# The second layer's injection multiplied inside the first layer norm, gelus by chunk, the context's first scale early, first weights ahead of the tokens

## The chip, the cores and the metric

The kernel runs on 1 core of one Trainium2 chip. The metric is the device time of one execution in microseconds (us), median of a few runs.

Names used below: PE is TensorE's matmul and PEld its weight load, DVE is VectorE, ACT is ScalarE, POOL is GpSimd, SP is SyncE, whose queue issues nearly all of the DMAs.

## What is computed

Two blocks follow one another. The first takes 256 tokens of width 1024 through four layers: a short convolution, a state-space scan (S5), an RWKV recurrence, and a convolution again. After each layer an injection of a second input `p` and a layer norm follow:

```python
def s5_mixer(x, ...):
    u, z = split(x @ w_in)                      # u feeds the scan, z a gate
    y = scan(u) + d_skip * u                    # 64 groups, 64 complex states each
    y = gelu(y)
    y = y * sigmoid(y @ w_glu + b_glu)
    return (y * silu(z)) @ w_out

def first_block(x, p, ...):
    for i in range(4):
        y = mixer[i](x)                         # conv, S5, RWKV, conv
        r = DN_ALPHA * x + y
        r = r + (p[i] @ ple_proj[i]) * sigmoid(r @ ple_gate[i])
        x = layer_norm(r, ln_g[i], ln_b[i])
    return x
```

The second block takes these tokens and a context of 256 tokens, which is an input of its own, through two layers. Each has a half feed-forward (FFN), a mixer in which tokens and context meet, and another half FFN. Each half FFN begins with an RMS norm that is modulated by numbers from a small vector product with `ada_w`:

```python
def half_ffn(h, g, shift, scale, gate, w1, w3, w2):
    hn = h * rsqrt(mean(h * h) + EPS) * g
    return h + 0.5 * gate * ((silu(mod(hn) @ w1) * (mod(hn) @ w3)) @ w2)
```

## The kernel before

**Layout.** Activations lie transposed: 1024 features are 8 chunks of 128 partitions, and the 256 tokens are the free dimension. A linear layer goes by tiles of 128 output features. Each tile has a weight block of 128 x 1024 fp32 (512 KB).

**Products.** An fp32 product is made from three reduced-precision ones: high by high, high by low, low by high. So a weight tile means 24 matmuls (8 chunks of input, 3 products) of 128 x 256. `Net.get` (L598 to L613) brings a weight block: a DMA on SP into the ring `w` of 4 buffers (L605), a copy `whi` on ACT (L606), a subtraction `wlo` on DVE (L607). Only `ssm_in` is left out of this and goes as raw fp32. Sums over features (means, variances) are matmuls with a constant matrix in `cs_base`, also raw fp32. `split` makes the high and low parts of an activation with one ACT and one DVE instruction.

**First block.** `conv` (layer 0) ends in `finish`, which makes `r` and its parts `rs`. Then `ple_norm` runs. It first calls `ple_proj(i)`: `p`'s two chunks are loaded and split, two weight blocks are fetched, and 48 matmuls (8 output chunks, 2 input chunks, 3 products) and 8 ACT copies make `pp`. It then goes through the 8 tiles of `ple_gate`, adds up `total`, takes the mean (`ps_st<-total`, `ps_st<-r`), subtracts it, squares (`sq`), takes the variance (`ps_st<-sq`), and writes the normed `x` (and for layers other than 0 its parts `xs`). Layer 0's call has a function `early`, which starts the phases of the scan (`ssm_m`, on ACT and DVE) while the norm runs.

**The scan.** `ssm` handles 8 chunks as groups, two at a time: a few matmuls (`ps_ca`, `ps_cb`), phase products and a scan on DVE, then matmuls into `ps_st`, and `y` on DVE. When all eight are done come the gelus of the 8 chunks (ACT, which loads a function table first), the splits into `ys_hi` and `ys_lo`, and the 8 tiles of `ssm_glu`.

**Side work and fillers.** Beside the main stream runs a side generator `n.side`: preparation of the scan, the load of the context, and `ada`, which fetches `ada_w` blocks through the same ring `w` and reduces each with one DVE instruction into `junk` (L1384). From the end of the scan on, the first FFN of the context (`ffn_in00`, `ffn_out`) is woven into the first block as filler: a tile of it (operands `h_hi`, `h_lo`, `d_hi`, `d_lo`) can run wherever the main stream waits. Its first step is `norm_mod`, with the squares of the context (`squares`), their sum, and `h_hi`, `h_lo`. After the first block the two streams, tokens and context, are woven together to the end.

**What sets the order.** The kernel plans itself: `weave` steps whichever stream is ready by a model of the engines' clocks (`Model`, `Engine`), with `yield` values as the expected delay of a step. The tile scheduler then orders the instructions of each engine by priority. Each engine, and SP's queue, runs its list in order.

Of the kernel before, what the change touches and what calls it, by code (L numbers as in the profile page):

```python
# [9 lines left out]
F32 = mybir.dt.float32  # L10
F32R = mybir.dt.float32r
# [8 lines left out]
S = 256  # L20
# [4 lines left out]
RAW = ("ssm_in",)  # L25

# [416 lines left out]
class Net:  # L443
    def __init__(self, tc, ap, pat, cat, es):
# [27 lines left out]
        self.sums = {}  # L472
        self.hold = 0
        self.fine = False
# [120 lines left out]
    def get(self, req):  # L595
# [3 lines left out]
        w = self.ws.tile([128, 1024], F32, name="w")  # L599
# [5 lines left out]
        nc.sync.dma_start(out=w[:, :n], in_=self.ap[name][i])  # L605
# [165 lines left out]
    def ple_proj(self, i):  # L771

        nc = self.nc
        raw = f"ple_proj{i}" in RAW
        t = self.slot(9, [2, 2, S], "p_split", F32 if raw else F32R)
        pp = self.slot(10, [NCH, S], "pp")
        for k in range(2):
            pf = t[:, 0, k] if raw else self.tmp("te")
            nc.sync.dma_start(out=pf, in_=self.ap["pT"][i][:, k])
            if not raw:  # L780
                self.split(pf, t[:, 0, k], t[:, 1, k])
        yield from self.linear(f"ple_proj{i}", t[:, 0] if raw else (t[:, 0], t[:, 1]), lambda m, ps: self.A.activation(out=pp[:, m], in_=ps, func=AF.Copy), 2, 4)
        return pp

    def ple_norm(self, R, i, split=True, free=2, early=None):
# [3 lines left out]
        pp = yield from self.ple_proj(i)  # L789
# [145 lines left out]
    def phases(self, c, q_, make):  # L935
# [4 lines left out]
        if q_ not in self.sets:  # L940
            self.sets[q_] = tuple(self.slot(k, [2048], f"ssm_m{k}") for k in ((6, 7), (0, 1))[q_])
# [20 lines left out]
    def ssm(self, X):  # L962
# [28 lines left out]
        y = full(10, "y")  # L991
# [3 lines left out]
        free = list(range(2))  # L995
        halves = lambda t: t.rearrange("p (t r) -> p r t", r=2)
# [3 lines left out]
        def group(c):  # L1000
# [37 lines left out]
            V.scalar_tensor_tensor(out=halves(y[:, c]), in0=halves(u[:, c]), scalar=self.p("ssm_d", c), in1=yp, op0=MUL, op1=ADD)  # L1038

# [7 lines left out]
        raw = "ssm_glu" in RAW  # L1047
        ys = y if raw else self.pair(0, 1, "ys")
        for c in range(NCH):
            self.tc.keep_in_program_order(self.act(y[:, c], y[:, c], AF.Gelu_apprx_tanh))  # L1050
            if not raw:
                self.split(y[:, c], ys[0][:, c], ys[1][:, c])
        yield 4.0
# [920 lines left out]
```

## Time and profile before

| | us |
|---|---|
| median of 3 runs | 2878.42 (2876.4 to 2881.57) |
| the profiled execution | 2878.2 |
| its span | 2876.3 |
| PE busy in the span | 2738.9 (95%) |
| DVE busy | 2130.2 (74%) |
| ACT busy | 1596.7 (56%) |

The profiled execution takes 1.9 us more than its span, and is 0.2 us under the median. PE is busy nearly all of the time, so the 137 us in which it is not, and the stretches in which it runs at half clock, are what there is to see. A busy time of PE counts a matmul from its start to its modelled end, so at half clock it is busy too. The slices of the page show where PE's share falls: at the start, around 170 to 330 us, and around 520 to 700 us.

### The profile page before, as it was taken

Reading aid. Unit: us, or ns where it says so; the run is one execution under the profiler, and the core shown is the slowest. Engines: PE = TensorE matmul, PEld = TensorE weight load, DVE = VectorE, ACT = ScalarE, POOL = GpSimd, SP = SyncE. Lnnn points to the kernel's source line nnn. Section 1 sums busy time; section 2 is a strip of 40 time slices with the busy share of each in tenths; the row PEclk is TensorE's granted clock in tenths of the full one; section 3 lists DMA queues with packets and bytes.
Section 4 is the critical chain, followed back from the end, with each engine's and each line's share of the span. In section 5 each row is a group of like instructions: output and inputs, shape, how many; then the busy total and the mean of one; then the engine's idle time right before and its main releaser. Section 6 shows DMA issues by size and latency. Waiting matters only on the chain.

```text
span 2876.3 us, 58509 instructions
## 1 busy us (share of the span) xinstructions
PE 2738.9 (95%) x23798; PEld 2587.5 (90%) x23798; DVE 2130.2 (74%) x3951; ACT 1596.7 (56%) x2946; POOL 13.0 (0%) x40
## 2 busy tenths in 40 slices
PE   8978799899999999999999999999999999999999
PEld 8967699778998998998999968999999999996999
DVE  8867777666688788898889887777854556676654
ACT  6455555866655465877666766545422234466443
POOL 0000000000000000000000000000000000000000
PEclk9989799999999999999999999999999999999999
DMA  7743355201486665666575644666544433322554
GB/s 273 244 158 111 107 169 176 82 17 41 159 263 226 221 200 176 211 215 202 182 231 186 201 134 150 209 219 208 176 140 133 132 112 109 94 91 62 160 183 140
DMA packets 132749, 467.51 MB, mean 163 GB/s; under 512 B 14720, under 2 KB 19072, under 8 KB 131840
## 3 DMA queue, kind: packets, MB, share of 16 engines
q1 hardware_dynamic: 132480, 463.78, 50.3%
q8 instruction: 187, 3.06, 0.4%
q14 instruction: 82, 0.67, 0.1%
HBM read 462.67 MB, written 1.05 MB: 161 GB/s over the span
## 4 chain that ended last, share of the span: by engine, by line
PE 68%; DVE 13%; DMA 9%; ACT 6%; issue 4%; SPq 0%; DVEq 0%; ACTq 0%
PE ps_mm L436 58%; DMA w<-in_ada_dram 6%; PE ps_ca L436 5%; DVE wlo L607 4%; PE ps_cb L436 2%; DVE junk L1384 2%; ACT whi L606 2%; DVE ssm_m L406 2%; PE ps_st L436 2%; DVE tc L406 1%; PE ps_cb L440 1%; DMA w<-in_ab_in_dram 1%; ACT rw_b L406 1%; ACT L406 1%; DMA w<-in_ffn_in_dram 1%
## 5 line engine op out<-in xcount | busy, mean ns | idle before, releaser
L606 ACT ACTIVATE whi<-w 128x1024 fp32r<-128x1024 f32 (+1 forms) x687 | 716.0, 1043 | 738.1 <-PE ps_mm L436 476.0
L607 DVE TENSOR_TENSOR wlo<-w,whi 128x1024 fp32r<-128x1024 f32 (+1 forms) x687 | 826.0, 1204 | 249.7 <-ACT whi L606 247.0
L436 PE MATMUL ps_mm<-h_hi,whi 128*128 128x256 f32 x3024 | 871.4, 290 | 16.8 <-ACT h_hi L406 12.9
L436 PE MATMUL ps_mm<-h_hi,wlo 128*128 128x256 f32 x3024 | 857.8, 285 | 6.0 <-DVE wlo L607 5.8
L436 PE MATMUL ps_mm<-h_lo,whi 128*128 128x256 f32 x3024 | 855.7, 284 | 1.1 <-DVE h_lo L406 1.0
L436 PEld LDWEIGHTS ps_mm<-h_hi,whi 128*128 128x128 f32 x3024 | 571.9, 190 | 27.2 <-ACT h_hi L406 16.4
L436 PEld LDWEIGHTS ps_mm<-h_lo,whi 128*128 128x128 f32 x3024 | 575.2, 190 | 6.0 <-DVE h_lo L406 2.8
L436 PEld LDWEIGHTS ps_mm<-h_hi,wlo 128*128 128x128 f32 x3024 | 572.8, 190 | 8.5 <-DVE wlo L607 7.8
L1384 DVE SCALAR_TENSOR_TENSOR junk<-w,cond 128x1024 bf16<-128x1024 f32 x288 | 351.7, 1221 | 149.9 <-DMA w<-in_ada_dram 148.8
L436 PE MATMUL ps_mm<-d_hi,whi 128*128 128x256 f32 x1232 | 355.5, 289 | 3.6 <-DVE ctx L406 2.7
L436 PE MATMUL ps_mm<-d_hi,wlo 128*128 128x256 f32 x1232 | 349.6, 284 | 0.6 <-DVE wlo L607 0.6
L436 PE MATMUL ps_mm<-d_lo,whi 128*128 128x256 f32 x1232 | 349.6, 284 | 0.4 <-DVE d_lo L406 0.4
L436 PEld LDWEIGHTS ps_mm<-d_hi,whi 128*128 128x128 f32 x1232 | 232.1, 188 | 8.0 <-issue 5.4
L436 PEld LDWEIGHTS ps_mm<-d_lo,whi 128*128 128x128 f32 x1232 | 233.3, 189 | 3.4 <-issue 1.2
L436 PEld LDWEIGHTS ps_mm<-d_hi,wlo 128*128 128x128 f32 x1232 | 232.6, 189 | 1.6 <-DVE wlo L607 0.8
L406 DVE TENSOR_TENSOR td<-td,ps_mm 128x256 f32<-128x256 f32 x154 | 64.4, 418 | 71.8 <-PE ps_mm L436 70.6
L406 ACT ACTIVATE d_hi<-td 128x256 fp32r<-128x256 f32 x154 | 63.1, 410 | 90.5 <-DVE td L406 89.7
L406 ACT ACT_TABLE_LOAD x80 | 102.6, 1283 | 2.1 <-PEq L1965 0.7
L436 PE MATMUL ps_mm<-x_hi,whi 128*128 128x256 f32 x256 | 73.9, 289 | 10.7 <-ACT whi L606 10.7
L406 ACT ACTIVATE tc<-tc 128x256 f32<-128x256 f32 x182 | 75.0, 412 | 5.2 <-DVE tc L406 2.4
L436 PE MATMUL ps_mm<-xs_hi,whi 128*128 128x256 f32 x256 | 73.3, 287 | 4.8 <-ACT xs_hi L406 4.6
L406 ACT ACTIVATE td<-ps_mm 128x256 f32<-128x256 f32 x154 | 57.4, 374 | 32.7 <-PE ps_mm L436 32.2
(466 smaller groups left out, 5233.8 us busy)
## 6 DMA issues: line engine op xcount, KB each, us to landing
w<-in_ffn_in_dram SPq DMA_DIRECT2D x268, 512.0 KB, 4.0
w<-in_ada_dram SPq DMA_DIRECT2D x168, 512.0 KB, 4.3
w<-in_ffn_out_dram SPq DMA_DIRECT2D x96, 512.0 KB, 4.0
w<-in_conv_in_dram SPq DMA_DIRECT2D x64, 512.0 KB, 4.7
w<-in_ffn_out_dram SPq DMA_DIRECT2D x48, 384.0 KB, 3.1
w<-in_ab_in_dram SPq DMA_DIRECT2D x34, 512.0 KB, 4.2
w<-in_ple_gate_dram SPq DMA_DIRECT2D x32, 512.0 KB, 4.3
w<-in_conv_out_dram SPq DMA_DIRECT2D x16, 512.0 KB, 4.8
```

Of the source, the lines that this page charges most:

```text
L406: return f(**kw)
L436: self.t.matmul(out, lhsT=lhsT, rhs=rhs, start=start, stop=stop)
L440: self.t.transpose(out, in_, ident)
L606: nc.scalar.activation(out=hi[:, :n], in_=w[:, :n], func=AF.Copy)
L607: nc.vector.tensor_tensor(out=lo[:, :n], in0=w[:, :n], in1=hi[:, :n].bitcast(F32), op=ALU.subtract)
L1384: nc.vector.scalar_tensor_tensor(out=self.junk, in0=w, scalar=1.0, in1=cb[:, s], op0=ALU.mult, op1=ALU.mult, accum_out=m[:, t, s:s + 1])
```

## The change

Five things are changed.

- `FIRST`: the DMA of the first weight block (`conv_in0`, tile 0) is issued ahead of the four DMAs of `x`.
- `ple_split` is taken out of `ple_proj`. In layer 0's norm (`early` is given) the injection of layer 1 is made: `p[1]` is split and its two weight blocks are fetched ahead of the mean, and the 48 matmuls and 8 copies into `pp` are emitted between the squares and the variance. Layer 1's `ple_norm` finds `pp` ready. Since `pp` then holds slot 10 during the scan, the scan's `y` takes the place of `u`, and the two sets of phase buffers swap places.
- The gelus and splits of the scan's result are emitted per chunk inside `group`, from the seventh finished chunk on.
- `context_scale` makes the context's first RMS scale in the side chain, ahead of `ada`: 8 squares on ACT, 8 raw fp32 matmuls against the mean matrix, the rsqrt. `norm_mod` uses it and leaves out its own squares and sums that first time.
- The output is stored by two DMAs, seven chunks and one, instead of one.

```diff
+FIRST = ("conv_in0", 0)
@@ get
-        w = self.ws.tile([128, 1024], F32, name="w")
+        w = self.ws.tile([128, 1024], F32, name="w") if not self.ahead else self.ahead.pop()
...
-        nc.sync.dma_start(out=w[:, :n], in_=self.ap[name][i])
+        if (name, i) != FIRST:
+            nc.sync.dma_start(out=w[:, :n], in_=self.ap[name][i])
@@ ple_norm
-        pp = yield from self.ple_proj(i)
+        pp = self.pp.pop(i) if i in self.pp else (yield from self.ple_proj(i))
...
         if early is not None:
             early()
+
+            ps_ = self.ple_split(i + 1)
+            ws = []
+            for b in range(2):
+                ws.append((yield (f"ple_proj{i + 1}", b, 2, 512)))
         yield 1.5
...
+        if early is not None:
+            self.pp[i + 1] = np_ = self.slot(10, [NCH, S], "pp")
+            for m in range(NCH):
+                ps = self.ps()
+                yield from self.mm3g(ps[:, :S], ws[m // 4], ps_, m % 4)
+                self.A.activation(out=np_[:, m], in_=ps[:, :S], func=AF.Copy)
         yield 3.5
@@ phases
-            self.sets[q_] = tuple(self.slot(k, [2048], f"ssm_m{k}") for k in ((6, 7), (0, 1))[q_])
+            self.sets[q_] = tuple(self.slot(k, [2048], f"ssm_m{k}") for k in ((0, 1), (6, 7))[q_])
@@ ssm
-        y = full(10, "y")
+        y = u
...
+            summed.append(c)
+
+            if len(summed) >= NCH - 1:
+                if not ys:
+                    ys.extend(self.pair(0, 1, "ys"))
+                for k in [k for k in summed if k not in gated]:
+                    gated.add(k)
+                    self.tc.keep_in_program_order(self.act(y[:, k], y[:, k], AF.Gelu_apprx_tanh))
+                    self.split(y[:, k], ys[0][:, k], ys[1][:, k])
...
-        ys = y if raw else self.pair(0, 1, "ys")
-        for c in range(NCH):
-            self.tc.keep_in_program_order(self.act(y[:, c], y[:, c], AF.Gelu_apprx_tanh))
-            if not raw:
-                self.split(y[:, c], ys[0][:, c], ys[1][:, c])
-        yield 4.0
+        yield 1.5
@@ context_scale, norm_mod
+        ms = self.ps("st")[:, :S]
+        for k in range(NCH):
+            t = self.tmp("tc")
+            self.A.activation(out=t, in_=self.ctx[:, k], func=AF.Square)
+            self.T.matmul(ms, lhsT=self.c("mean"), rhs=t, start=k == 0, stop=k == NCH - 1)
+        rs = self.few.tile([128, S], F32, name="rs")
+        self.V.tensor_copy(out=rs, in_=self.rsqrt(ms, 1e-6))
+        self.rs[1] = rs
...
+        if s in self.rs:
+            rs = self.rs.pop(s)
+            self.hold += 1
+        else:
...
@@ program
+        n.ahead = [n.ws.tile([128, 1024], F32, name="w")]
+        nc.sync.dma_start(out=n.ahead[0], in_=ap[FIRST[0]][FIRST[1]])
         X = Stream(n, n.first())
...
-        n.side = itertools.chain(n.ssm_prep(), load_context(), n.ada(c, [(0, i, (1,), GAPS[0] / 2) for i in range(PARTS)]))
+        n.side = itertools.chain(n.ssm_prep(), load_context(), n.context_scale(), n.ada(c, [(0, i, (1,), GAPS[0] / 2) for i in range(PARTS)]))
...
-        nc.sync.dma_start(out=out, in_=x)
+        nc.sync.dma_start(out=out[:, :7], in_=x[:, :7])
+        nc.sync.dma_start(out=out[:, 7:], in_=x[:, 7:])
```

Since the planner's clocks see other costs, the order of the engines' lists changes in more places than the diff. Three of them matter below.

PE's list in layer norm 0. The last products of `ple_gate0` (`rs_hi`, `rs_lo`) stand ahead of the mean (`total`, `r`), the variance (`sq`) and the first raw matmuls of `ssm_in` (`x,w`). Before:

```order
L436 MATMUL ps_mm<-rs_lo,whi 128x256
L436 MATMUL ps_mm<-rs_hi,wlo 128x256
L436 MATMUL ps_st<-total,cs_base 128x256
L436 MATMUL ps_st<-r,cs_base 128x256
L436 MATMUL ps_st<-sq,cs_base 128x256 x3
L436 MATMUL ps_mm<-x,w 128x256 x12
```

After, the same place:

```order
L437 MATMUL ps_mm<-rs_hi,wlo 128x256
L437 MATMUL ps_mm<-p_split,whi 128x256 x2
L437 MATMUL ps_mm<-p_split,wlo 128x256
L437 MATMUL ps_mm<-p_split,whi 128x256 x2
L437 MATMUL ps_st<-total,cs_base 128x256
L437 MATMUL ps_mm<-p_split,wlo 128x256
L437 MATMUL ps_mm<-p_split,whi 128x256 x2
L437 MATMUL ps_mm<-p_split,wlo 128x256
L437 MATMUL ps_mm<-p_split,whi 128x256 x2
```

Five matmuls of the injection now stand ahead of `total`, 25 between `total` and `r`, and 18 between `r` and `sq`.

ACT's list at the end of the scan. `sz` is the scan's gate, `tc` a temporary of the context's norm, `y` (after: `u`) the scan's result under gelu. Before:

```order
L406 ACTIVATE sz<-ps_mm 128x256
L406 ACTIVATE squares<-ctx 128x256 x8
L397 ACT_TABLE_LOAD
L406 ACTIVATE tc<-ps_mm,fixed_66 128x256
L406 ACTIVATE tc<-tc 128x256 x2
L406 ACTIVATE h_hi<-tc,mod 128x256 x8
L406 ACT_TABLE_LOAD
L406 ACTIVATE y<-y 128x256
L406 ACT_TABLE_LOAD
L406 ACTIVATE td<-ps_mm 128x256
L406 ACTIVATE ys_hi<-y 128x256
L406 ACT_TABLE_LOAD
```

After:

```order
L407 ACTIVATE h_hi<-tc,mod 128x256 x3
L407 ACTIVATE sz<-ps_mm 128x256
L407 ACT_TABLE_LOAD
L407 ACTIVATE u<-u 128x256
L407 ACTIVATE ys_hi<-u 128x256
L407 ACTIVATE u<-u 128x256
L407 ACTIVATE ys_hi<-u 128x256
```

The squares are gone from here, three of the context's eight `h_hi` stand ahead of the gelus, and the pairs of gelu and split follow one another eight times with one table load ahead of them.

SP's list over the scan's end, from the raw weights of `ssm_in` on. Before:

```order
L601 DMA w<-in_ssm_in_dram 128x1024 x16
L1381 DMA w<-in_ada_dram 128x1024 x2
L605 DMA w<-in_ffn_in_dram 128x1024
L605 DMA w<-in_ssm_glu_dram 128x1024 x7
L513 DMA rwkv_c<-in_const_rwkv_dram 128x1088
L605 DMA w<-in_ssm_glu_dram 128x1024
L605 DMA w<-in_ffn_in_dram 128x1024 x2
```

After:

```order
L603 DMA w<-in_ssm_in_dram 128x1024 x16
L1401 DMA w<-in_ada_dram 128x1024
L608 DMA w<-in_ssm_glu_dram 128x1024
L1401 DMA w<-in_ada_dram 128x1024
L608 DMA w<-in_ssm_glu_dram 128x1024 x2
L1401 DMA w<-in_ada_dram 128x1024
L608 DMA w<-in_ssm_glu_dram 128x1024 x2
L1401 DMA w<-in_ada_dram 128x1024
L515 DMA rwkv_c<-in_const_rwkv_dram 128x1088
L608 DMA w<-in_ssm_glu_dram 128x1024 x2
L1401 DMA w<-in_ada_dram 128x1024
L608 DMA w<-in_ssm_glu_dram 128x1024
```

Five blocks of `ada` instead of two now stand among the `ssm_glu` weights, in the ring of four that both share.

## Rows read from the trace of the kernel before

**Rows 1.** The page: busy time by engine, and the weights' low part on DVE.

```profile
PE 2738.9 (95%) x23798; PEld 2587.5 (90%) x23798; DVE 2130.2 (74%) x3951; ACT 1596.7 (56%) x2946; POOL 13.0 (0%) x40
...
L607 DVE TENSOR_TENSOR wlo<-w,whi 128x1024 fp32r<-128x1024 f32 (+1 forms) x687 | 826.0, 1204 | 249.7 <-ACT whi L606 247.0
```

**Rows 2.** Windows (stretch and its us, busy by engine, granted clock, DMA share, GB/s).

```profile
102.30:171.60 69.30, 67.58 (x553) 66.76 (x551) 54.13 (x94) 32.64 (x53) 0.10 (x1) 0.98 0.71 235
171.60:193.00 21.40, 5.00 (x10) 2.90 (x10) 15.08 (x37) 13.14 (x31) 0.00 (x0) 0.68 0.39 129
...
303.00:327.30 24.30, 16.75 (x113) 12.33 (x105) 14.62 (x31) 13.22 (x25) 4.45 (x9) 0.57 0.08 24
...
868.60:885.10 16.50, 10.42 (x77) 9.65 (x77) 14.37 (x34) 11.43 (x23) 0.00 (x0) 0.93 0.64 213
1110.00:1800.00 690.00, 671.57 (x5046) 619.00 (x5046) 601.25 (x1177) 484.85 (x852) 0.00 (x0) 0.99 0.60 190
```

**Rows 3.** Timeline of the start (start, us, engine, what, idle before and its releaser).

```profile
0.74 1.81 SPq L712 DMA_DIRECT2D x<-in_xT_dram  x4
...
9.60 1.06 ACT L606 ACTIVATE whi<-w 128x1024 fp32r<-128x1024 f32 x1 [0.70 <-DMA w<-in_conv_in_dram]
...
10.71 0.58 PE L436 MATMUL ps_mm<-x_hi,whi 128*128 128x256 f32 x1 [10.71 <-ACT whi L606]
```

**Rows 4.** Timeline of PE in layer norm 0.

```profile
177.98 1.22 PE L436 MATMUL ps_st<-total,cs_base 128*128 128x256 f32 x2 [6.39 <-DVE total L406]
178.99 1.06 PE L436 MATMUL ps_st<-r,cs_base 128*128 128x256 f32 x2
186.66 2.93 PE L436 MATMUL ps_st<-sq,cs_base 128*128 128x256 f32 x6 [6.61 <-DVE sq L406]
193.03 5.19 PE L436 MATMUL ps_mm<-x,w 128*128 128x256 f32 x15 [3.44 <-ACT x L406]
```

**Rows 5.** Windows in layer norm 0 and at the scan's end, columns as above.

```profile
176.20:180.20 4.00, 2.07 (x4) 1.06 (x4) 3.23 (x9) 0.63 (x1) 0.00 (x0) 0.51 0.87 295
...
193.00:196.70 3.70, 3.67 (x9) 2.94 (x10) 2.20 (x6) 2.77 (x7) 0.00 (x0) 0.54 0.00 0
...
313.30:321.00 7.70, 7.53 (x24) 5.72 (x24) 5.91 (x14) 4.81 (x10) 0.00 (x0) 0.50 0.01 2
321.00:327.20 6.20, 3.30 (x12) 2.71 (x12) 1.95 (x4) 6.10 (x11) 0.00 (x0) 0.50 0.00 0
327.30:329.80 2.50, 2.50 (x11) 2.50 (x12) 1.51 (x5) 2.40 (x8) 0.00 (x0) 0.50 0.62 198
329.80:334.00 4.20, 4.20 (x36) 4.20 (x36) 1.28 (x3) 2.21 (x5) 0.00 (x0) 0.99 0.02 9
```

**Rows 6.** The chain of waits around layer 1's injection (start, us, what).

```profile
371.99 18.05 PE ps_mm L436 x149
```

**Rows 7.** The chain of waits at the end of the scan.

```profile
308.23 1.65 PE ps_mm L436 x4
...
319.25 1.28 ACT L406
320.54 0.01 issue
320.55 0.42 ACT y L406
...
327.29 4.74 PE ps_mm L436 x28
```

**Rows 8.** DMA issues: count, KB each, median us to landing.

```profile
w<-in_ssm_glu_dram SPq DMA_DIRECT2D x8, 512.0 KB, 3.7
...
p<-in_cd_bias_dram SPq DMA_DIRECT2D x16, 128.0 KB, 2.1
...
out_dram<-x SPq DMA_DIRECT2D x1, 1024.0 KB, 3.9
```

**Rows 9.** The chain of waits in the third layer norm.

```profile
874.88 0.45 PE ps_st L436 x2
...
879.20 3.60 DMA w<-in_conv_in_dram
```

More of the change, by code (lines that the diff above doesn't have):

```diff
@@ L471, in __init__ @@
         self.parts, self.stage = [[0, 0], [0, 0]], ""
-        self.sums = {}
+        self.sums, self.rs = {}, {}
         self.hold = 0
+        self.pp = {}
         self.fine = False
@@ L773, in ple_proj, with ple_split @@
         nc = self.nc
-        raw = f"ple_proj{i}" in RAW
-        t = self.slot(9, [2, 2, S], "p_split", F32 if raw else F32R)
+        t = self.ple_split(i)
         pp = self.slot(10, [NCH, S], "pp")
+        yield from self.linear(f"ple_proj{i}", t, lambda m, ps: self.A.activation(out=pp[:, m], in_=ps, func=AF.Copy), 2, 4)
+        return pp
+    def ple_split(self, i):
+        t = self.slot(9, [2, 2, S], "p_split", F32R)
         for k in range(2):
-            pf = t[:, 0, k] if raw else self.tmp("te")
-            nc.sync.dma_start(out=pf, in_=self.ap["pT"][i][:, k])
-            if not raw:
-                self.split(pf, t[:, 0, k], t[:, 1, k])
-        yield from self.linear(f"ple_proj{i}", t[:, 0] if raw else (t[:, 0], t[:, 1]), lambda m, ps: self.A.activation(out=pp[:, m], in_=ps, func=AF.Copy), 2, 4)
-        return pp
+            pf = self.tmp("te")
+            self.nc.sync.dma_start(out=pf, in_=self.ap["pT"][i][:, k])
+            self.split(pf, t[:, 0, k], t[:, 1, k])
+        return t[:, 0], t[:, 1]
     def ple_norm(self, R, i, split=True, free=2, early=None):
@@ L1046, in ssm @@
         yield 1.0
-        raw = "ssm_glu" in RAW
-        ys = y if raw else self.pair(0, 1, "ys")
-        for c in range(NCH):
-            self.tc.keep_in_program_order(self.act(y[:, c], y[:, c], AF.Gelu_apprx_tanh))
-            if not raw:
-                self.split(y[:, c], ys[0][:, c], ys[1][:, c])
-        yield 4.0
+        yield 1.5
         g = self.operand("ssm_out", (2, 3), "g")
@@ L1062, in take_g @@
             self.put(g, m, th, lambda o: V.scalar_tensor_tensor(out=o, in0=th, scalar=0.5, in1=sz[:, m], op0=MUL, op1=MUL))
-        yield from self.linear("ssm_glu", ys, take_g)
+        yield from self.linear("ssm_glu", tuple(ys), take_g)
         yield 1.5
@@ L1401, in modulation, with context_scale @@
                 yield Until(self.now() + 2.0)
+    def context_scale(self):
+        ms = self.ps("st")[:, :S]
[6 more added lines that the diff above has]
+        self.rs[1] = rs
+        yield 3.0
     def norm_mod(self, l, g, i, x, s):
@@ L1408, in norm_mod @@
         self.V.scalar_tensor_tensor(out=ga, in0=self.mod[:, l, (i + 1) * NCH:(i + 2) * NCH, s], scalar=1.0, in1=self.p("norm_g", (l * 3 + g) * NCH, NCH), op0=ALU.add, op1=ALU.mult)
-        if s not in self.sums:
-            for k in range(NCH):
-                self.square(s, k, x[:, k], 4 * s + 2)
-            yield 2.5
-        sq = self.sums.pop(s)
-        ms = self.bsum(self.c("mean"), lambda k: sq[:, k * (NCH - 1)], 2)
-        rs = self.rsqrt(ms, 1e-6)
+        if s in self.rs:
+            rs = self.rs.pop(s)
+            self.hold += 1
+        else:
+            if s not in self.sums:
+                for k in range(NCH):
+                    self.square(s, k, x[:, k], 4 * s + 2)
+                yield 2.5
+            sq = self.sums.pop(s)
+            ms = self.bsum(self.c("mean"), lambda k: sq[:, k * (NCH - 1)], 2)
+            rs = self.rsqrt(ms, 1e-6)
         hi, lo = self.pair(4 * s, 4 * s + 1, f"h{s}")
```

1 line of the change is left out of this document (added).

## The prediction

> **What bounds the kernel now.** The busy times come first: PE is busy 95% of the span, DVE 74% [rows 1]. Of 2876.3 us PE is idle 137, so a change pays in three ways: it takes matmuls away, it fills a gap of PE with matmuls that are done later now, or it spares PE a stretch at half clock, which counts as busy. The windows come second, because the average hides where these gaps lie [rows 2]: 16.4 us of 21.4 in layer norm 0, 7.6 of 24.3 at the scan's end, 6.1 of 16.5 in the third norm, but only 1.7 of 69.3 ahead of norm 0 and 18.4 of 690 in the large woven stretch after 1110 us. The granted clock is the other half: at the scan's end it is 0.50 (1.2 GHz) from 313.3 to 329.8 us, although PE is busy most of that time, and full (2.4 GHz) right after [rows 5]. The chain of waits then says what the gap is made of: at the scan's end the context's norm, the function tables and the gelus stand one behind another from 308.2 to 327.3 us [rows 7].
>
> At full clock the chain shows 149 matmuls back to back in 18.05 us [rows 6]: 0.121 us each, 2.9 us for a weight tile of 24. At half clock 11 of them fill 2.50 us [rows 5]: 0.23 us each.
>
> **The change part by part**, against the profiled execution's 2878.2 us (the median of the runs is 0.2 us above it).
>
> *First weights ahead.* Before, the first matmul starts at 10.71 us, waiting for `whi`, which waits for the weight's DMA; that DMA stands on SP behind the 1.81 us of `x`'s issues [rows 3]. Ahead of them it can land up to 1.8 us earlier, and `whi` (1.06 us) no longer stands at the end of the start; `x` itself lands later, and the next weights come no sooner. Ends: -2.9 and 0. I take -1.9.
>
> *Context's scale early.* It adds eight raw fp32 matmuls. The nearest row is a mean's pair of records, 0.45 us [rows 9], so 8 x 0.45 = 3.6 us. The order of PE puts them between the tiles of `conv_out`, a stretch with 1.7 us of idle in 69.3 [rows 2], so little covers them. Ends: 0 (they fall into waits for weights) and +3.6; I take +3.0. The eight squares on ACT are free there: ACT is busy 32.64 of 69.30 us.
>
> *The injection inside norm 0.* Removed: 48 matmuls at 0.121 = 5.8 us, from a stretch in which PE has no gap at all [rows 6], so all of it counts. The two weight blocks move along, and that only helps the later stretch. Added: the same 48 in norm 0, whose idle 16.4 us could hold them even at half clock (48 x 0.23 = 11.0). But PE takes its list in order, and 25 of them stand between the two halves of the mean, which in the profile of before follow one another [rows 4]. The mean, and all that hangs on it (centring, squares, variance), comes later by 25 x 0.121 = 3.0 to 25 x 0.23 = 5.8 us; the middle is 4.4. ACT is busy 13.14 of 21.40 us there, much of it with the scan's phases, which can go ahead while the mean is late; I let half be absorbed: +2.2. The eight copies into `pp` are some 0.42 us each (the ACT step of the same 128 x 256 shape in [rows 7]); the order leaves three of them between the last square and the logarithm's table load: at most 1.3, taken as 0.8. Against that, a PE that has worked may keep its clock. The variance's 2.93 us and the first 3.7 us of `ssm_in` run at 0.50 and 0.54 of the clock before [rows 4, 5]; at full clock they would be 1.5 and 1.8 us shorter. I take -1.0 of these. So norm 0 grows by 2.0 and the part is -5.8 + 2.0 = -3.8; ends -9.1 (everything warm, nothing late) and +1.3.
>
> *Gelus by chunk, and the context's norm off the end of the scan.* Before, PE's last group ends at 308.2 us and from there to 329.8 us it does the context's sums, then 24 + 12 + 11 = 47 matmuls, all at half clock [rows 5, 7]: 24 of the context's tile, 23 of `ssm_glu`. After, seven of eight chunks have passed gelu when the last group ends, and some of the context's operands are ready, so these 47 can follow at once. With 3.7 us at half clock first, as `ssm_in` needs after norm 0 [rows 5], that is 16 matmuls, and 31 more at 0.121: 7.5 us in all, done at 315.7 instead of 329.8. That is -14.1; with a warm PE it is 5.7 us and -15.9. What is late next is a weight. Five blocks of `ada` now stand among those of `ssm_glu` in the ring of four, and each frees its buffer only after a DVE step that queues behind the scan on DVE. A step of this ring in the open is: the DVE step (1.2 us; the row of `wlo`, same tile, taken for it), landing 3.7 [rows 8], `whi` 1.06 [rows 3], `wlo` 1.2 [rows 1]: 7.2 us, of which one tile of 2.9 covers part. I count one such exposure, 4.3, since four blocks can be there before the need begins: -14.1 + 4.3 = -9.8. Ends: -15.9 and, with all of the last four tiles exposed, +3.
>
> Here the trace speaks against a page. A table load takes 1.28 us and the next ACT instruction starts 0.02 us behind it [rows 7]. The Trainium skill (page "ScalarE: Activation LUTs", section "What ACT_TABLE_LOAD costs") adds a drain of about 1.38 us to each, 2.66 in all. The order of ACT has two loads fewer in this place; by the page they would save another 2 x 1.38 = 2.8 us and the forecast would be some 2857. By the row they save nothing beyond what the -14.1 holds, and I go by the row.
>
> *More filler done early.* The order now holds one context tile more in the RWKV scan (-2.9) and two more in the third norm (-5.8, against 6.1 us of idle there [rows 2]). But there the first `conv_in` weights are split only after the normed operands; before, a weight's landing (3.60 us, [rows 9]) and `whi` (1.06) lay among the norm's steps. If they come into the open, that is +4.7. Net -4.0; ends -8.7 and +4.7.
>
> *Output in two.* The last transfer shrinks from 1024 KB, 3.9 us, to 128 KB, for which the nearest row has 2.1 us [rows 8]. The large part starts a tile (2.9 us) earlier and is over. -1.8; ends -2.0 and 0.
>
> *The woven rest.* Its order changes in many places but the work is the same. PE idles 18.4 us in its largest stretch [rows 2], which a re-ordering can give or take in part: 0, ends -8 and +8.
>
> Sum: -1.9 + 3.0 - 3.8 - 9.8 - 4.0 - 1.8 + 0 = -18.3, so 2878.2 - 18.3 = 2859.9, say 2860 us. Taken together (root of squares of the half-widths, about 14), the ends give 2846 to 2874.
>
> **The rivals.**
>
> *The gain is given back.* The ring behind `ada` exposes each of the last four `ssm_glu` tiles (4 x 4.3 = 17.2, so that part gives +3 instead of -9.8): 2860 + 13 = 2873. If the weave returns a few microseconds as well, up to 2880. For it: DVE is the one that frees the ring and is the scan's own engine. Against it: 47 matmuls of cover stand ready, and the context's tiles can run in between. About no change.
>
> *Slower through the large woven stretch.* With four to five context tiles done before it instead of about two, the context's and the token stream's serial steps (norms, attention) may come at the same time, with no filler left for either. PE is busy 671.57 of 690 us there and DVE 601.25 [rows 2]; a DVE at 87% can become the bound in parts. It ends slower than before once that stretch loses over 24 us (18.3 + 5.8), 3.5% of it; at 5%, 34 us, the time is 2894. For it: DVE's share. Against it: the fillers that are missing there were done in idle time earlier, so the stretch has less work by the same amount.
>
> *The injection does not pay.* The mean is late by the whole 5.8 us with nothing absorbed, and the clock stays at half: norm 0 grows by 7.1, the part is +1.3 instead of -3.8: 2865.
>
> *More than forecast.* PE stays warm from norm 0 on and no weight is exposed: -5.3 in norm 0, -6.1 at the scan's end: 2849.
>
> **How the numbers follow.** Chances: the forecast 0.45, the injection that doesn't pay 0.15, more than forecast 0.13, given back 0.17, slower through the weave 0.10. About 0.2%, 5.8 us, is what a measurement of this kernel tells from no change: faster means under 2872.7, slower over 2884.2. So faster 0.73, same 0.17, slower 0.10. The range of 8 in 10 leaves out the slower case and a part of the ends: 2844 to 2877.
>
> **What would show each step.** Norm 0: `ps_st<-r` behind 25 matmuls of `p_split`, ending near 184 us rather than 180, and `ssm_in` starting about 195 at a higher clock. At 380 us no matmuls of `p_split`. The scan's end: no stretch of 16 us at 0.50; the first `ssm_glu` matmuls ahead of the last group; PE's waits for `wlo` of `ssm_glu` at most one of about 4 us. The third norm: more matmuls between its mean and its variance. The end: the last store lands about 2 us after its issue. The forecast is wrong if the offset between equal instructions of the two traces, about 14 us at the first `ssm_out` tile and about 20 at the end of the third norm, shrinks again after 1110 us; or if PE waits for several `ssm_glu` weights in a row.

## The result, and the profile after

The changed kernel takes 2860.32 us (median of four runs, 2859.29 to 2864.55), the kernel before 2879.99 us beside it: a ratio of 0.9931, with a 95% interval of 0.9911 to 0.9951. The forecast was 2860.0. The execution that was profiled is the slowest of the four, 2864.55 us, of which the span is 2862.7: 13.6 us shorter than that of before, where the medians differ by 19.7.

The page's busy times hardly move against [rows 1]; PE is idle 127 us of the span instead of 137:

```profile
PE 2735.5 (96%) x23810; PEld 2589.5 (90%) x23810; DVE 2128.4 (74%) x3947; ACT 1591.5 (56%) x2944; POOL 13.0 (0%) x40
```

The start, in order of time, answers to [rows 3]. The first matmul comes at 6.90 instead of 10.71 us and waits for the tokens' split `x_hi`, no longer for the weight:

```profile
0.74 0.38 SPq L1949 DMA_DIRECT2D w<-in_conv_in_dram  x1
1.18 1.84 SPq L715 DMA_DIRECT2D x<-in_xT_dram  x4
...
4.33 1.06 ACT L609 ACTIVATE whi<-w 128x1024 fp32r<-128x1024 f32 x1 [2.32 <-DMA w<-in_conv_in_dram]
...
6.90 0.58 PE L437 MATMUL ps_mm<-x_hi,whi 128*128 128x256 f32 x1 [6.90 <-ACT x_hi L407]
```

PE in layer norm 0, which answers to [rows 4]. The injection (`p_split`, not shown) fills the stretch from `total` to `r`, which is now 4.43 us long instead of 1.01; the trace has 21 of its matmuls there and 22 behind `r`, where 25 and 18 were read from the order; the variance (`sq`) still takes 2.93 us:

```profile
172.88 0.70 PE L437 MATMUL ps_st<-total,cs_base 128*128 128x256 f32 x2 [2.51 <-DVE total L407]
...
177.31 0.71 PE L437 MATMUL ps_st<-r,cs_base 128*128 128x256 f32 x2
185.95 2.93 PE L437 MATMUL ps_st<-sq,cs_base 128*128 128x256 f32 x6 [5.20 <-DVE sq L407]
```

The scan's end, in windows with the columns of [rows 2]: layer norm 0 first, then the end of the raw weights, and then two stretches that answer to [rows 5]. Before, the granted clock was 0.50 (1.2 GHz) for 16.5 us there; now PE is full and at full clock (2.4 GHz) from 310 to 322 us:

```profile
169.80:192.30 22.50, 11.37 (x58) 9.72 (x57) 14.44 (x37) 16.82 (x40) 0.00 (x0) 0.75 0.34 121
...
291.30:310.00 18.70, 10.87 (x165) 8.23 (x166) 18.13 (x39) 9.59 (x24) 4.45 (x9) 0.73 0.23 75
310.00:322.00 12.00, 12.00 (x102) 12.00 (x101) 11.81 (x25) 7.57 (x15) 0.00 (x0) 1.00 0.46 143
322.00:334.30 12.30, 10.90 (x75) 10.30 (x74) 10.40 (x19) 6.55 (x12) 0.96 (x1) 0.87 0.74 233
```

The chain of waits there answers to [rows 7] (start, us, what). Norm, tables and gelus are gone from it. What stands in it is one weight of `ssm_glu`, issued only when a `wlo` on DVE has ended:

```profile
307.82 11.36 PE ps_mm L437 x93
...
320.12 1.23 DVE wlo L610
...
321.40 5.29 DMA w<-in_ssm_glu_dram
...
328.81 1.23 DVE wlo L610
```

The RWKV scan, from its first matmul to the first of `rwkv_out`, before and then after, the same columns. It holds 22 weight tiles of the context before and 23 after:

```profile
524.30:807.70 283.40, 266.69 (x3858) 230.90 (x3857) 188.18 (x432) 181.47 (x467) 1.10 (x1) 0.98 0.24 78
```

```profile
508.10:799.70 291.60, 273.49 (x3883) 236.47 (x3882) 189.05 (x435) 187.70 (x474) 1.10 (x1) 0.97 0.24 79
```

It is 8.2 us longer, and one tile of 24 matmuls explains 2.9 of these.

The chain at the end of the third norm answers to [rows 9]: it goes through the first `conv_in` weight and both of its splits. The landing stood on the chain before, too.

```profile
878.88 3.50 DMA w<-in_conv_in_dram
...
882.46 1.06 ACT whi L609
...
883.55 1.24 DVE wlo L610
```

The end. The last two stores and how long they take (KB, median us from issue to landing), against 1024 KB in 3.9 us [rows 8]:

```profile
out_dram<-x SPq DMA_DIRECT2D x1, 896.0 KB, 3.8
out_dram<-x SPq DMA_DIRECT2D x1, 128.0 KB, 2.0
```

**The leads.** The table gives how many us earlier than in the trace of before the same place is reached, at equal work: 2.9 us are added for each tile of the context that is done more by then, and taken off for each done less. e1 is a second run of the changed kernel; the other columns are the experiments below. The trace of before belongs to a run of 2878.2 us, and the kernel before has a median of 2875.9 to 2879.2 in the later comparisons, so that leads at the end exceed the timed gains by up to 2.3 us for that alone.

| place | after | e1 | e2 | e3 | e4 | e5 | e8 | e10 | e11 |
|---|---|---|---|---|---|---|---|---|---|
| `ple_gate0` over | 1.8 | 0.0 | 2.4 | 1.1 | 1.4 | 0.9 | 1.1 | 1.0 | 4.8 |
| `ssm_in` begins | 0.7 | 1.6 | 1.8 | 2.0 | -2.0 | -1.3 | -1.1 | -1.4 | 4.5 |
| `ssm_in` over | 0.2 | 2.0 | 1.7 | 2.1 | -2.4 | -0.5 | -0.1 | -1.4 | 5.4 |
| second norm's mean | 18.7 | 22.9 | 0.4 | 18.6 | 14.4 | 13.8 | 19.6 | 18.2 | 25.2 |
| RWKV scan begins | 19.0 | 22.1 | 0.6 | 18.7 | 14.2 | 12.7 | 19.5 | 18.0 | 24.9 |
| `rwkv_out` begins | 13.8 | 16.0 | 0.3 | 14.3 | -2.3 | 8.4 | 12.0 | 18.0 | 24.1 |
| second `conv_in` over | 13.6 | 20.1 | 1.7 | 17.9 | -0.6 | 12.0 | 10.1 | 22.1 | 25.3 |
| end | 13.6 | 22.0 | 1.3 | 19.6 | 4.2 | 15.5 | 10.3 | 23.2 | 32.6 |

### The profile page after: what moved, and what is told of

It is laid out like the page before. It is cut to its first block, busy times and chain, and to the rows that moved or that the text cites. A ratio compares the mean times of both kernels' runs of the same rounds, so it can differ in the third digit from the quotient of the medians.

```text
span 2862.7 us, 58511 instructions
## 1 busy us (share of the span) xinstructions
PE 2735.5 (96%) x23810; PEld 2589.5 (90%) x23810; DVE 2128.4 (74%) x3947; ACT 1591.5 (56%) x2944; POOL 13.0 (0%) x40
## 4 chain that ended last, share of the span: by engine, by line
PE 66%; DVE 14%; DMA 9%; ACT 7%; issue 4%; SPq 0%; ACTq 0%; DVEq 0%
PE ps_mm L437 55%; PE ps_ca L437 5%; DMA w<-in_ada_dram 4%; DVE wlo L610 4%; PE ps_cb L437 3%; ACT whi L609 2%; PE ps_st L437 2%; DVE junk L1404 2%; DVE ssm_m L407 2%; DVE tc L407 2%; DMA w<-in_ffn_in_dram 1%; DMA w<-in_conv_in_dram 1%; PE ps_cb L441 1%; ACT tc L407 1%; ACT L407 1%
## 5 line engine op out<-in xcount | busy, mean ns | idle before, releaser
L437 PE MATMUL ps_mm<-h_hi,whi 128*128 128x256 f32 x3024 | 871.8, 289 | 13.8 <-ACT h_hi L407 5.7
L437 PEld LDWEIGHTS ps_mm<-h_hi,wlo 128*128 128x128 f32 x3024 | 571.4, 189 | 10.1 <-DVE wlo L610 9.6
L437 PE MATMUL ps_mm<-xs_hi,wlo 128*128 128x256 f32 x256 | 74.0, 289 | 3.7 <-DVE wlo L610 3.7
```

Of the source, the lines that this page charges most:

```text
L437: self.t.matmul(out, lhsT=lhsT, rhs=rhs, start=start, stop=stop)
```

## The experiments

Each ratio is to the kernel before, on the same chip and beside it, with its 95% interval.

**e1, the changed kernel once more**, with no edit.

> The changed kernel, unaltered, for a second profile: the profiled execution (2864.5 us) lay 4 us above the median of its runs (2860.3). Theory: the planned order is the same, so the first block runs alike to within 1 us (first matmul 6.9 us, last matmul of ssm_glu 334.3, first of rwkv_out 799.7, variance of the fourth norm 1049.1) and the 4 us arise after 1110 us, where two streams share the weights' ring; ratio to the kernel before 0.9931 again. Rival: the first block itself differs by some us between executions, for instance in the RWKV stretch, and then the 10.7 us that the change's lead loses there (508 to 800 us) is partly chance: rwkv_out would start 3 us or more earlier than 799.7.

0.9932 [0.9915, 0.9949], 2855.86 against 2876.01 us. The gain repeats. But two executions of the same lists of instructions differ by 4.2 us of lead at the second norm, so a lead of one execution is good to about that; the theory had expected the first block alike to within 1 us. The loss in the RWKV scan repeats: 6.1 us of lead against 5.2.

**e2, only the two ends**: the kernel before with the first weight ahead and the output in two.

```diff
+FIRST = ("conv_in0", 0)
...
+        n.ahead = [n.ws.tile([128, 1024], F32, name="w")]
+        nc.sync.dma_start(out=n.ahead[0], in_=ap[FIRST[0]][FIRST[1]])
...
-        nc.sync.dma_start(out=out, in_=x)
+        nc.sync.dma_start(out=out[:, :7], in_=x[:, :7])
+        nc.sync.dma_start(out=out[:, 7:], in_=x[:, 7:])
```

> The kernel before with the two ends of the change alone: first weight block issued ahead of the tokens, output stored by two transfers. The planner sees neither, so every engine's order stays that of before. Theory: the start's gain (3.2 us through conv_in in the changed kernel, where 1.9 was forecast) and the end's (2.2 us, where 1.8 was forecast) are real and add: conv_in's tiles begin 3.2 us earlier all the way to 85 us, the last store is 3.0 us ahead of the span's end instead of 5.2, and the time falls by 5.4 us (ratio 0.998). Rival: the start's lead is spent where weights are late anyway (conv_out and norm 0 in the changed kernel kept only 0.7 us of lead), so that only the end's 2.2 us stay: ratio 0.9992.

0.9993 [0.998, 1.0005], 2873.12 against 2876.01 us: not to be told from nothing, and near the rival's 0.9992. The lead of 2.4 us at the end of `ple_gate0` is 0.4 at the second norm: what the start gains is gone by the end of the selective scan.

**e3, the injection back in layer 1's norm.**

```diff
-            ps_ = self.ple_split(i + 1)
-            ws = []
-            for b in range(2):
-                ws.append((yield (f"ple_proj{i + 1}", b, 2, 512)))
...
-        if early is not None:
-            self.pp[i + 1] = np_ = self.slot(10, [NCH, S], "pp")
-            for m in range(NCH):
-                ps = self.ps()
-                yield from self.mm3g(ps[:, :S], ws[m // 4], ps_, m % 4)
-                self.A.activation(out=np_[:, m], in_=ps[:, :S], func=AF.Copy)
```

> The changed kernel with the injection of layer 1 made in its old place (the first step of layer 1's norm), all else as changed. Theory: the 48 matmuls cost their full 5.8 us there (layer 1's first gate matmul loses 5.7 us of its lead) and layer norm 0 gives back about 1 us, so up to the second layer norm the kernel stands 4.6 us behind the changed one; the planner then also places fewer early tiles of the context (40, 43 and 45 by the third and fourth norm instead of 44, 47 and 49), which costs some us more. Ratio to before 0.9945 to 0.996. Rival: the injection's 5.8 us reappear as waits anyway, the lead of the changed kernel is lost in the RWKV stretch, and the time is within 2 us of the changed one (0.993).

0.9946 [0.9927, 0.9964], 2860.63 against 2875.89 us: 4.0 us of gain less than e1 by the ratios (0.0014 x 2876), though the intervals overlap. The traces do not settle what the move is worth. The removed matmuls show in full: between the last product of `ssm_out` and the first of `ple_gate1` lie 5.7 us before and 5.8 in e3, and nothing in after (366.0 and 365.9 us). But from the end of `ssm_in` to that last product e3 gains 16.4 us, where the changed list gains 12.8, 15.3, 14.0 and 14.0 (after, e1, e8, e10), and e3 passes norm 0 0.9 us faster than before, the changed list mostly 1.1 to 2.4 slower. So at the second norm e3 leads by 18.6 us and the changed list by 18.7, 22.9, 19.6 and 18.2: 1.2 us more in the mean, less than two executions differ by. Behind it the RWKV scan has another order in e3 as well (287.8 us for 22 tiles).

**e4, without the early context scale.**

```diff
-        n.side = itertools.chain(n.ssm_prep(), load_context(), n.context_scale(), n.ada(...))
+        n.side = itertools.chain(n.ssm_prep(), load_context(), n.ada(...))
```

> The changed kernel without the context's early scale: the squares, their sum and the norm of the context come back to the scan's end, the gelus by chunk stay. Theory: conv_out ends 2.4 to 3.4 us earlier (the eight raw matmuls are gone); at the scan's end the gelus by chunk alone let ssm_glu start at once, so its last matmul keeps at least 10 of the 13 to 17 us that the changed kernel gains there; but the context's tiles come 3 fewer before the second norm (1 and 3 instead of 4 and 7), and since early tiles fill idle time the kernel is 3 to 8 us slower than the changed one: ratio to before 0.994 to 0.996. Rival: the scale alone carries the gain at the scan's end, since the context's norm stood ahead of the gelus on ACT: ssm_glu's last matmul falls back by 8 us or more.

0.9995 [0.9983, 1.0007], 2874.41 against 2875.89 us. The whole gain is gone, but not at the scan's end: there (from `ssm_in` over to the second norm) e4 still gains 16.8 us, 2.9 less than the changed list's mean of 19.7 (18.5, 20.9, 19.7 and 19.6 in after, e1, e8 and e10). Two places elsewhere take it. Norm 0 costs 3.4 us. And the RWKV scan, with the 22 tiles of before, is 16.5 us longer than before:

```profile
501.40:801.30 299.90, 272.79 (x3859) 234.62 (x3858) 189.44 (x435) 197.65 (x481) 1.10 (x1) 0.97 0.22 73
```

So this ratio, outside the expected 0.994 to 0.996, is no price of the scale alone. The planner sees other costs and writes another order of the RWKV scan, and that order is the worst one seen.

**e5, the gelus after the whole scan.**

```diff
-            summed.append(c)
-            if len(summed) >= NCH - 1:
...
+        ys.extend(self.pair(0, 1, "ys"))
+        for c in range(NCH):
+            self.tc.keep_in_program_order(self.act(y[:, c], y[:, c], AF.Gelu_apprx_tanh))
+            self.split(y[:, c], ys[0][:, c], ys[1][:, c])
+        yield 4.0
```

> The changed kernel with the gelus and splits after the whole scan again, the context's scale still early. The planner's count of early context tiles stays that of the changed kernel (38, 44, 47, 49). Theory: eight pairs of gelu and split at 0.755 us follow one table load of 1.28 us behind the last group, while a context tile or two runs: the last matmul of ssm_glu comes 3 to 6 us later than in the changed kernel, at 334 to 337 us, and the time rises by as much (ratio to before 0.9945). Rival: the gelus by chunk are the whole gain at the scan's end: the last ssm_glu matmul is back near 345 us or later, and the ratio at 0.997 or more.

0.9952 [0.9937, 0.9967], 2862.75 against 2875.89 us. From the end of `ssm_in` to the second norm it gains 14.3 us (13.8 of lead, with 0.5 of arrears to begin with) instead of 19.7: the gelus by chunk are worth 5.4 there. The last `ssm_glu` matmul ends at 342.2 us, between the 334 to 337 of the theory and the 345 of the rival. Its chain does not go through gelus with table loads between them, as that of before does [rows 7], but through short handovers (one `whi`, one `ys_hi`) between groups of PE:

```profile
313.37 0.80 PE ps_mm L437 x4
...
314.18 1.06 ACT whi L609
315.24 0.31 ACT ys_hi L407
...
315.60 1.99 PE ps_mm L437 x6
```

**e7, the mean first**: the changed kernel, with the injection's 48 matmuls kept behind both halves of the mean on PE, the variance kept behind the injection in the same way (not shown), and the copies into `pp` on DVE.

```diff
+        after_mean = self.T.last.ins
...
+                with self.tc.issue_after(after_mean):
+                    yield from self.mm3g(ps[:, :S], ws[m // 4], ps_, m % 4)
+                self.V.tensor_copy(out=np_[:, m], in_=ps[:, :S])
-                yield from self.mm3g(ps[:, :S], ws[m // 4], ps_, m % 4)
-                self.A.activation(out=np_[:, m], in_=ps[:, :S], func=AF.Copy)
```

> The changed kernel with another order in layer norm 0 alone: the 48 matmuls of the injection stand behind both halves of the mean on PE (before, 21 of them ran between), and their copies into pp are made by DVE instead of ACT. Every other list is as in the changed kernel. Theory: the mean waits 1.2 to 1.6 us for the injection's matmuls there (PE takes up the second half at 177.3 us, DVE had its operand ready at 175.8), and ACT's copies lie among the squares; so ssm_in starts 1 to 2 us earlier than 192.3 and the whole kernel is 1 to 2 us faster (ratio to the changed kernel 0.9995). Rival: the phases of the scan on ACT, not the mean, set the variance; the mean comes earlier, the squares wait for ACT all the same, and ssm_in starts within 0.5 us of 192.3.

0.9921 [0.9907, 0.9936], 2852.55 against 2876.01 us: 3.3 us below e1 by the medians, with intervals that overlap. PE in norm 0:

```profile
173.72 1.22 PE L437 MATMUL ps_st<-total,cs_base 128*128 128x256 f32 x2 [2.88 <-DVE total L407]
176.69 1.22 PE L437 MATMUL ps_st<-r,cs_base 128*128 128x256 f32 x2 [1.74 <-DVE r L407]
186.05 1.46 PE L437 MATMUL ps_st<-sq,cs_base 128*128 128x256 f32 x6
```

With nothing ahead of it, `r` still starts only at 176.69 and waits for DVE. So the injection held up the mean's second half by little (1.5 to 1.6 us in after, e5, e8 and e10, 0.1 in e1); mostly DVE, with two `junk` steps between `total` and the last `r`, sets it. The order also gains at the variance: it follows matmuls, runs at full clock and takes 1.46 us instead of 2.93, though it starts 9.4 us behind `r` instead of 8.6 in after. Norm 0 is 1.4 us faster than before; with the same order it is 0.5 faster in e9 and 0.3 slower in e11.

**e8, fillers as before**: the changed kernel with the context held at 36 tiles until the RWKV layer is over, which is the count of before.

```diff
-            live = [s for s in streams if not s.done and not s.blocked()]
+            live = [s for s in streams if not s.done and not s.blocked() and not (self.stage == "rwkv" and s.got >= s.cap)]
...
+        C.cap = 36
```

> The changed kernel, but the context's stream is stopped at 36 weight tiles until the RWKV layer is over, as many as the kernel before has done there; after that the planner again places 40, 42 and 44.3 tiles by the marks at which the kernel before has them (the changed kernel: 38 in the RWKV layer, then 44, 47, 49). All else stays. Theory one (the forecast's): tiles done early fill idle time, so without them the time rises by about 4 us, the term of the forecast: ratio to before 0.9945. Theory two: in these stretches PE is busy anyway, the early tiles cost their full 2.9 us each where they are put, and only the place changes: rwkv_out starts 5 us or more earlier than 799.7, the fourth norm 9 to 14 us earlier than 1042, and the end is the same within 2 us (ratio 0.993). Theory three: the early tiles cost more than they save, by finer interleaving and later weights: the time falls by 3 us or more (ratio 0.992 or less).

0.9973 [0.9963, 0.9982], 2867.75 against 2876.01 us, worse than the changed kernel and than all three theories had it. Its RWKV scan takes 288.0 us for 21 tiles, 7.5 us more than before at equal work. The number of fillers is therefore not what lengthens that scan.

**e9, e7 with the context's squares summed on DVE**, so that PE does one raw product instead of eight.

```diff
-            self.T.matmul(ms, lhsT=self.c("mean"), rhs=t, start=k == 0, stop=k == NCH - 1)
+            if k:
+                self.V.tensor_tensor(out=acc, in0=acc, in1=t, op=ALU.add)
+        self.T.matmul(ms, lhsT=self.c("mean"), rhs=acc, start=True, stop=True)
```

> The changed kernel with the new order in layer norm 0 (mean ahead of the injection on PE, copies by DVE, as in the run that had this alone and ended 3.3 us faster than the changed kernel) and with the context's squares added on DVE, so that one raw matmul pair stands in conv_out instead of eight. Theory: conv_out ends 2 to 3 us earlier (7 x 0.43 us of PE saved in a stretch where PE is busy over 92%), and about half of it survives to the end: 4 to 6 us faster than the changed kernel, ratio to before 0.991 to 0.992. Rival: conv_out waits for weights behind ada (its `w` ring), not for PE; the 3 us are lost there or at the scan's end, where the start's lead of 3 us also shrank to 0.4 us: the same as with the new order alone, 0.992.

0.9912 [0.9897, 0.9927], 2851.12 against 2875.89 us. `conv_out` is over 2.9 us earlier than before. In the seven runs with the eight raw products its end lies between 0.8 us earlier and 1.1 later (after and e1 are the two ends), in the four without them (e2, e4, e9, e11) 1.9 to 4.7 earlier: the eight raw products did lie in the open there. In time e9 and e7 can't be told apart.

**e10, the RWKV scan in the order of before**: the changed kernel with the context held at 14 tiles (the count of before) until that scan begins. From `ple_gate1` on, every engine's list is then word for word that of before, but for the split output.

```diff
+            live = [... and not (self.capped and s.got >= s.cap)]
...
         self.drain()
+        self.capped = False
...
+        C.cap = 14
```

> The changed kernel with one edit: the context's stream may take at most 14 weight tiles until the RWKV scan begins (the kernel before has 14 there, the changed kernel 15). From layer 1's gate on, every engine's list is then word for word that of the kernel before, to the end of the program, but for the store in two parts; the changed parts ahead of it stay. Theory: the changed kernel's lead (about 19 to 23 us at the second layer norm) shrank by 5 to 6 us between the RWKV scan's start and rwkv_out because the planner wove that stretch in another order (292 us for 23 tiles instead of 283 us for 22), by chance and not by a cost of the change; in the order of before the stretch takes 283 to 285 us again, the lead of 19 to 23 us stays to the end, and the time is 20 to 25 us under before: ratio 0.9915 to 0.993, as good as or better than the changed kernel although 5 fewer tiles are done early. Rival one: a lead is lost in the RWKV stretch whatever its order (the start of it is bound by a serial chain or by the context's tiles running out): the stretch takes 288 us or more and the lead at rwkv_out is 15 us or less, ratio 0.995. Rival two: the lead holds through the RWKV stretch but shrinks after it, since the five tiles that the changed kernel had done early by 1049 us (14 us of PE) are missing later: ratio 0.994 to 0.996 with a full lead at rwkv_out.

0.9921 [0.9905, 0.9937], 2856.00 against 2879.17 us. The scan:

```profile
506.30:789.80 283.50, 265.94 (x3859) 230.50 (x3858) 189.56 (x435) 182.53 (x468) 1.10 (x1) 0.98 0.24 79
```

It takes the 283.5 us of before, and the lead of 18.0 us at its start is 18.0 at its end and 22.1 after the second `conv_in`. So it is the order of its lists that lengthened it, and nothing that the earlier stages leave behind: e11, with these lists too, takes 284.2 us. In time this is no worse than the changed kernel (0.9921 against 0.9932, overlapping).

**e11, e9 and e10 together.**

> The same edit together with the new order in layer norm 0 and the context's squares added on DVE (the run with those two alone stood at 0.9912). Theory: 3 to 5 us under the run with the edit alone, ratio 0.990 to 0.9915, and the lead at the second layer norm 1 to 2 us larger than there. Rival: the planner's order of the changed kernel in the RWKV stretch and after, with five tiles more done early, is worth more than the order of before: slower than 0.9912.

0.9888 [0.9871, 0.9904], 2847.24 against 2879.17 us, 31.9 us less, and 8.8 less than e10, where 3 to 5 were expected. Its interval lies below those of both runs of the changed kernel and of every experiment but e9. It keeps a lead of 24 to 26 us from the second norm to the second `conv_in`.

## Why the prediction held, point by point

The sum of the forecast, put on the same stretches as the leads (minus is time saved):

| stretch | forecast | after | e1 |
|---|---|---|---|
| start to `ple_gate0` over: first weight -1.9, scale +3.0 | +1.1 | -1.8 | 0.0 |
| layer norm 0: injection, copies, clock | +2.0 | +1.1 | -1.6 |
| `ssm_in` | 0 | +0.5 | -0.4 |
| to the second norm: injection removed -5.8, gelus and context's norm -9.8 | -15.6 | -18.5 | -20.9 |
| to the RWKV scan | 0 | -0.3 | +0.8 |
| RWKV scan: a tile more for nothing | -2.9 | +5.2 | +6.1 |
| to the second `conv_in` over: third norm -5.8, weights +4.7 | -1.1 | +0.2 | -4.1 |
| to the end: output -1.8, woven rest 0 | -1.8 | 0.0 | -1.9 |
| sum | -18.3 | -13.6 | -22.0 |

The time is right, and the two largest errors have opposite signs: the scan's end gave 3 to 5 us more than forecast, the RWKV scan took 8 to 9 us more. So that the total came out to the microsecond is in part a cancellation, which is luck.

*First weights.* Right in direction, too small, and of no use in the end. PE starts 3.8 us earlier, beyond the -2.9 taken as the bound. That bound counted only the issues that the weight is moved past (its own comes 1.85 us earlier), but its `whi` starts at 4.33 instead of 9.60 us. Yet e2 shows 2.4 us left after `ple_gate0` and 0.4 at the second norm.

*Context's scale.* +3.0, which was within its ends. e9 takes most of it away and ends `conv_out` 2.1 us earlier than after and 4.0 earlier than e1, so a price of that size is paid there. At the end of `ple_gate0` less is left: the leads with the scale are 0.0 to 1.8, against 2.4 in e2 and 1.4 in e4 without it.

*Norm 0.* The size was right, the reason was not. Six executions (after, e1, e4, e5, e8, e10) have the injection between `total` and `r`; norm 0 grows in them by +1.1, -1.6, +3.4, +2.2, +2.2 and +2.4, with the middle at 2.2 against 2.0 forecast. The step that failed is "25 of them stand between the two halves of the mean ... comes later by 3.0 to 5.8 us". From the last product of `ple_gate0` to `r` it takes 7.4 us before, and 7.5, 4.7, 8.5, 8.5 and 8.8 in after, e1, e5, e8 and e10; only e4 has 10.7. In after DVE had `r` ready at 175.79 (175.37 + 0.42, below) and PE took it at 177.31, 1.5 us late; up to there DVE sets the mean, as e7 confirms.

What grew in all but e4 is the stretch from `r` to `sq`: 8.6 to 8.8 us against 7.7 before. ACT's list has a table load there, behind copies into `pp`, which before has not and which the forecast did not count. DVE's `r` and then ACT, in after:

```profile
175.37 0.42 DVE L407 SCALAR_TENSOR_TENSOR r<-ta,r 128x256 f32<-128x256 f32 x1
```

```profile
177.13 0.38 ACT L407 ACTIVATE pp<-ps_mm 128x256 f32<-128x256 f32 x1 [0.90 <-PE ps_mm L437]
177.53 1.28 ACT L407 ACT_TABLE_LOAD   x1
178.82 0.63 ACT L407 ACTIVATE ssm_m<-ssm_m 128x512 f32<-128x512 f32 x1
```

e4 has the same copies without this load, and takes 7.8 us from `r` to `sq`. That the load makes the difference is the reading that fits; it was not tried by itself. The copies behind the last square, taken as 0.8, cost nothing: from `sq` to `ssm_in` it is 6.4 us before and in all six. The part taken for the clock, -1.0, came only in e7: the variance is at 2.93 us in all six, 1.46 in e7, and in after the first 3.7 us of `ssm_in` run at 0.50. So the signs named for this stage failed as well: `r` ends at 178.0 us and not near 184, and `ssm_in` starts at 192.3 and not about 195, at no higher clock.

*The injection's net.* -3.8 forecast, 4.0 us by the ratios of e3 and e1, whose intervals overlap. The removed 5.8 us show in full, but up to the second norm the net is only 1.2 us in the mean (e3), within the chance of single executions. So neither its sign nor its size is shown, and the rival by which it doesn't pay (a cost of 1.3 us) is not excluded.

*The scan's end.* The mechanism was right; the term was mis-sized: -9.8 against 18.5 - 5.8 = 12.7 and 20.9 - 5.8 = 15.1 measured. The forecast counted 3.7 us at half clock, and one weight in the open at 4.3 us. In after the weight costs about 12.3 - 10.9 = 1.4 us of idle time and some more at a lower clock (0.87, the last of the windows above). In e1 that stretch has neither:

```profile
308.00:330.20 22.20, 21.37 (x177) 21.10 (x177) 21.07 (x43) 14.02 (x25) 0.96 (x1) 1.00 0.62 196
```

So it came near the warm end, -15.9. Of the mean of 13.9 us (19.7 less 5.8), 5.4 go when the gelus are put back (e5), 2.9 when the scale is (e4), and the other 5.6 stay as long as one of the two is there. The drain of about 1.38 us that the Trainium skill (page "ScalarE: Activation LUTs", section "What ACT_TABLE_LOAD costs") adds to each table load doesn't show here either: the load ahead of the gelus starts at 293.20 us and lasts 1.28, and the first gelu starts at 294.50.

*More filler early.* This is the step that failed. "The order now holds one context tile more in the RWKV scan (-2.9)" takes the tile to fit into idle time with the rest of the scan unchanged. But the planner wrote the whole scan anew, and at equal work it lost 5.2 and 6.1 us. e8 (21 tiles, 7.5 us lost), e3 and e4 (22 tiles, 4.4 and 16.5 lost) and e10 (22 tiles, nothing lost) show that the order decides and not the count. What in the order costs the time stays open. How often PE's list changes between scan and filler does not explain it: 95 times before and 115 after, but 97 in e3 and only 85 in e4, the slowest. In the windows of before and after PE's busy time grows by 6.8 us, where a tile explains 2.9, and its idle time by 1.4; the granted clock is 0.98 and 0.97. No run tells apart which of the interleavings does it. The third norm with its weights went much as forecast in after (+0.2 against -1.1): from the norm's mean to the first `conv_in` matmul the lead grows by 4.5 us, against 5.8 taken for the filler, and 4.9 are lost again by the end of `conv_in`, against 4.7 taken for the weights. But only 1.4 of the 4.9 go in the first two tiles, and [rows 9] shows that weight's landing on the chain before as well, not among the norm's steps, so the reason given for the 4.7 is not shown. In e1 the whole did better (4.3 gained, 3.1 lost, and 2.9 gained ahead of the mean).

*Output.* -1.8 forecast. From the last step of DVE to the end of the span it is 5.2 us before and 3.0 after: -2.2. The Trainium skill (page "DMA: Bandwidth & Descriptors", section "Bandwidth") advises batching transfers to 1 MiB or more. That is a rule for throughput; for the last store of this kernel the time to landing counts, and the measurement decides against it: 3.9 us for 1024 KB, 2.0 for 128 KB. The runs' times do not show these 2 us by themselves (e2).

*The woven rest and the rivals.* After the second `conv_in` little is given back (0.0 in after, 1.9 gained in e1, the output's 2.2 included, so 2.2 and 0.3 lost), so the rival of a slower woven stretch at 1110 us and beyond, which asked for over 24 us, falls. "Given back" came true in another place than it named: not the ring behind `ada` but the RWKV scan took 5 to 6 us. The forecast's spread was added up a little small: the root of the squares of its half-widths is 15.2 us, not about 14.

## What to carry to other kernels

Where a planner orders the lists, a local change is not local: before costing a tile more or less in a later stage, compare that stage's lists with those of before, and if they differ, count on several us either way or pin the order (here e10 and e11, which pin it by holding back the fillers). A matmul stage put into a norm costs little where another engine sets the norm's steps, but look at what its copies bring onto that engine, a table load for instance; and it should stand where it fills the wait ahead of the next sum, not between two halves of one. The last part of an output should be small, and gains at the very start of a program have to be followed to the next stage that waits for something else.

## What the runs showed of the chip that was not expected

Executions with the same lists in layer norm 0 differ there by up to 4 us, and the wait ahead of `total` goes with it. In the five of them PE had idled 1.00, 2.51, 3.36, 3.44 and 3.64 us before `total` (e1, after, e5, e8, e10), and norm 0 grew by -1.6, +1.1, +2.2, +2.2 and +2.4, in the same order. (In e4, without the table load, it was 4.61 us and +3.4.) Part of this is the idle time itself, and part the clock behind it. The windows from `total` to `r`, in after and then in e1, the clock being the third number from the end:

```profile
173.20:177.30 4.10, 4.10 (x23) 4.07 (x22) 3.27 (x8) 1.22 (x4) 0.00 (x0) 0.61 0.74 242
```

```profile
173.20:176.30 3.10, 3.10 (x24) 3.05 (x25) 3.10 (x7) 1.85 (x5) 0.00 (x0) 1.00 0.83 246
```

After 2.51 us of idling the granted clock is 0.61, after 1.00 us it is 1.00, and about as many matmuls take 4.1 us in the one and 3.1 in the other. Over these five, 1 us more of idling ahead of the sum goes with 1.5 us more of norm 0 (4.0 us over 2.64). That the idle time causes the lower clock is the reading that fits them; it was not tried by itself.
